# Pools and shared banks of the w_in stage divided by the end of their tiles, a bias added as columns, and gMLP transfers issued by GpSimd

## The chip, the cores and the metric

The kernel runs on one core of one Trainium2 chip. A core has TensorE (PE: matmuls and transposes into PSUM, eight banks of 2 KB per partition), VectorE (DVE), ScalarE (ACT), GpSimd (POOL) and SyncE (SP, which here only issues DMAs). The engines run side by side, each in its own program order; an instruction whose input or space isn't ready holds everything behind it on its engine. The metric is the device time of one execution in microseconds (us). A program's time is the median of its runs.

## The reference, cut to what matters

One layer over two token streams, 512 latent tokens and 128 context tokens, which the kernel holds as one block of T = 640 columns; a flag v (0 latent, 1 context) says which of two modulation vectors applies.

```python
mod = silu(c) @ w_mod + b_mod                       # once for c, once for c_ctx; six vectors of 2048
sh1, sc1, g1, sh2, sc2, g2 = split(mod, 6)
h = rmsnorm(x, norm1_g) * (1 + sc1) + sh1
p = h @ w_in                                        # 2048 x 5408
o_a = rwkv7_bidir(shift(p[..., :3360]))             # two delta-rule scans, 16 heads of 64
u, v = split(gelu(p[..., 3360:]), 2)                # gMLP, 8 groups of 128
v = layernorm_of_group(v) * gmlp_ln_g + gmlp_ln_b
o_b = u * (w_spatial @ v + b_spatial)
x = x + g1 * (concat(o_a, o_b) @ w_out)
h = rmsnorm(x, norm2_g) * (1 + sc2) + sh2
y = rmsnorm(x + g2 * ((silu(h @ w_gate) * (h @ w_up)) @ w_down), final_norm_g)
```

Results: the two streams after the last norm, and the context scan's final states. All is float32; large matmuls take each operand as a high and a low part and add three products.

## The kernel before, in words

Every array is transposed: 128 features on the partitions, 640 tokens along the row. The stages, in order of time: normalisation and the first two modulation vectors; **w_in**; **w_out** together with the scans (the recurrence over chunks of 64 tokens, one "hop" after another); the feed-forward layer in two stages (each a Strassen scheme of seven products in place of eight); the last norm.

*The w_in stage* (from about 150 us) makes 43 column blocks of p, 128 columns each, the first six already in the stage before. A block is four pieces of weights (raw, 256 KB each); each is cut into hi (ACT) and lo (DVE) and multiplied with h_hi and h_lo in groups of three matmuls of 320 columns into two of the three banks called big. `wide[0]` counts these groups: 192 at the stage's start, 1376 at its end. A finished block is copied to one of four buffers praw and goes to a generator: `take_r`, `take_v`, `take_k` prepare the scans, then `tail`, `solve` and `merge` invert the small triangular matrices of a head pair and direction (tiles TB, TF, M1, M2, A1_; PE's pblk, pM2, pT2) and store them with the scan's records in d_S; `take_gv` and `take_gu` make a gMLP group (lng, lnb, wsp, bsp are its loads; its product goes to d_o). `mod_all` makes the other four modulation vectors beside them: for each vector 16 pieces of 1 MB of weights (wt, through one buffer mraw), each multiplied in four matmuls of two rows (pm); piece n isn't let go before `wide[0]` is 192 + MODR * n. When 16 pieces are summed, ms (in the same buffer) is cleared by POOL, takes b_mod by eight DMAs, DVE adds the sums, PE transposes (ptm), and DVE copies the result to modc.

All these operations are recorded first (class `Op`, whose call is line 106, so that the stage's rows in the profile bear L106). `Lister` then writes them out: it keeps a clock for each engine, takes operations whose inputs are ready by its own estimates, and among them the task with the lower number of priority (gMLP and modulation have 5, the last). The order on each engine is fixed by this, including SP's DMAs. When w_in's products are all listed, the rest is written in a second run, `plan.run(last=True)`, outside the fixed order: the framework merges these instructions with those of the next stage by its own estimates.

*Space.* Tiles come from pools, and a pool has one piece of memory. When a stage's pools are closed, the next stage's pools lie in the same memory, and a tile there waits for the last user of every pool that it overlaps, not only of the tile that lay at its place. In w_in all working tiles of the left side are in three pools: bk, bp and gs; the four banks of its small PE results (slots, tags g0 to g3, used for pblk, psp, ptm and the like) are one pool pk; the modulation's bank is a tile of pm_. In w_out the space of bk, bp and gs is taken by x1T (the residual, loaded transposed by PE's pxT and then added to), by ol and oh (low and high part of d_o) and, over h_hi and h_lo, by the scan's records rec; the banks of pk by the pools pu, po (pxT's) and py.

*The w_out stage* here begins with the gMLP half: `wout_b` loads ol for rows 8 to 11 of d_o, then for each of 16 output tiles two half products of 12 matmuls (L1305 to L1307, banks pbig, two of them), which DVE adds onto x1T times the vector g1 (modc[2], L1318).

## Time and profile before

| | us |
|---|---|
| median of three runs | 3212.35 (3209.28 to 3218.95) |
| the profiled execution's own time | 3210.99 |
| its span, first to last instruction | 3209.2 |
| mean granted TensorE clock | 0.984 |
| PE busy | 3097.7 (97% of the span) |
| weight loads of PE | 2878.0 (90%) |
| DVE busy | 2328.3 (73%) |
| ACT busy | 1448.3 (45%) |
| POOL busy | 1256.2 (39%) |

Busy times say little of a stage: the prediction below reads the profile by stretches of time. A row of the time order gives start, duration, engine, line, operation, the tile written <- the tiles read, sizes and a count, and in brackets how long the engine stood idle before it and what ended that. "SPq" is a DMA issue on SP's queue.

### The profile page before, as it was taken

The page shows a single profiled execution, that of the slowest core. Times are in us where ns is not written, and L with a number is a line of the kernel's source. Part 1 is how long each engine was busy: PE and PEld are TensorE (multiplying, and loading weights), DVE is VectorE, ACT ScalarE, POOL GpSimd, SP SyncE. Part 2 cuts the span into 40 slices and gives each one's busy share as a digit, 9 for nine tenths or more (in the row PEclk, how much of TensorE's full clock was granted, in tenths as well). Part 3 has the DMA queues.
Part 4 walks back from the last instruction along what each step waited for, and adds up shares of the span by engine and source line. Part 5 has one row for each costly group of instructions (what it writes and reads, how often), then busy time and mean ns, then how long its engine had stood idle before and what let it go on. Part 6 is the DMA issues. An engine that isn't in the chain of part 4 may idle for free. (4 is left out here: it accounts for less than half of the span.)

```text
span 3209.2 us, 73753 instructions
## 1 busy us (share of the span) xinstructions
PE 3097.7 (97%) x28892; PEld 2878.0 (90%) x28892; DVE 2328.3 (73%) x4118; ACT 1448.3 (45%) x3169; POOL 1256.2 (39%) x1102
## 2 busy tenths in 40 slices
PE   7999999999997999999899999999999999999996
PEld 4888888888885877799899999999999999999996
DVE  5567676866765667557887777877778777877787
ACT  4245454555543433346544444444444444444365
POOL 1001222222220123210465666566656645555543
PEclk9999999999997999999999999999999999999998
DMA  9768888788797677356334334434343354554453
GB/s 349 241 186 245 207 228 229 200 239 228 193 249 236 205 226 240 116 156 187 100 119 126 118 109 129 126 108 123 118 123 120 107 183 145 169 164 130 124 171 122
DMA packets 746412, 553.02 MB, mean 172 GB/s; under 512 B 142128, under 2 KB 682768, under 8 KB 737232
## 3 DMA queue, kind: packets, MB, share of 16 engines
q1 hardware_dynamic: 733104, 534.52, 56.1%
q0 software_dynamic: 10624, 13.23, 1.8%
q8 instruction: 227, 3.72, 0.5%
q14 instruction: 121, 0.99, 0.1%
q10 hardware_dynamic: 2336, 0.57, 0.1%
HBM read 438.77 MB, written 111.69 MB: 172 GB/s over the span
## 5 line engine op out<-in xcount | busy, mean ns | idle before, releaser
L1875 PE MATMUL P<-xo,lo 128*128 128x320 f32 x2352 | 728.2, 310 | 7.5 <-DVE lo L1663 7.5
L1873 PE MATMUL P<-xo,hi 128*128 128x320 f32 x2352 | 728.1, 310 | 2.2 <-ACT hi L1662 2.2
L1874 PE MATMUL P<-xo,hi 128*128 128x320 f32 x2352 | 728.1, 310 | 0.0
L1663 DVE TENSOR_TENSOR lo<-raw,hi 128x512 fp32r<-128x512 f32 x532 | 504.3, 955 | 172.7 <-ACT hi L1662 170.9
L1662 ACT CAST hi<-raw 128x512 fp32r<-128x512 f32 x532 | 330.3, 622 | 505.5 <-PE P L1874 434.1
L1875 PEld LDWEIGHTS P<-xo,lo 128*128 128x128 f32 x2352 | 442.7, 188 | 8.0 <-DVE lo L1663 8.0
L1873 PEld LDWEIGHTS P<-xo,hi 128*128 128x128 f32 x2352 | 442.6, 188 | 2.4 <-ACT hi L1662 2.4
L1874 PEld LDWEIGHTS P<-xo,hi 128*128 128x128 f32 x2352 | 442.6, 188 | 0.0
L1773 POOL TENSOR_TENSOR raw<-raw 128x512 f32<-128x512 f32 x252 | 412.8, 1641 | 17.3 <-DVE lo L1663 4.1
L1875 PE MATMUL P<-xd,lo 128*128 128x320 f32 x1232 | 383.5, 311 | 5.6 <-DVE lo L1663 5.6
L106 PE MATMUL big<-h_hi,hi 128*128 128x320 f32 x1184 | 387.7, 327 | 0.7 <-DVE early L580 0.7
L1873 PE MATMUL P<-xd,hi 128*128 128x320 f32 x1232 | 383.3, 311 | 5.2 <-ACT P L2171 3.1
L1874 PE MATMUL P<-xd,hi 128*128 128x320 f32 x1232 | 382.1, 310 | 0.1
L106 PE MATMUL big<-h_lo,hi 128*128 128x320 f32 x1184 | 364.5, 308 | 0.0
L106 PE MATMUL big<-h_hi,lo 128*128 128x320 f32 x1184 | 364.4, 308 | 0.0
L1773 POOL TENSOR_TENSOR t<-raw 128x512 f32<-128x512 f32 x84 | 134.3, 1598 | 460.2 <-DMA raw<-in_w_ffn_up_dram 366.7
L1662 ACT CAST hi<-rawd 128x512 fp32r<-128x512 f32 (+1 forms) x288 | 165.0, 585 | 229.9 <-PE P L1874 144.4
L106 PEld LDWEIGHTS big<-h_hi,hi 128*128 128x128 f32 x1184 | 222.5, 188 | 35.4 <-issue 28.7
L1663 DVE TENSOR_TENSOR lo<-rawd,hi 128x512 fp32r<-128x512 f32 (+1 forms) x288 | 217.7, 764 | 49.4 <-ACT hi L1662 47.1
L1873 PEld LDWEIGHTS P<-xd,hi 128*128 128x128 f32 x1232 | 232.6, 189 | 8.8 <-ACT P L2171 5.6
L1875 PEld LDWEIGHTS P<-xd,lo 128*128 128x128 f32 x1232 | 232.4, 189 | 8.7 <-DVE lo L1663 8.4
L1874 PEld LDWEIGHTS P<-xd,hi 128*128 128x128 f32 x1232 | 232.6, 189 | 0.3 <-DVE xd L1926 0.3
(402 smaller groups left out, 6413.2 us busy)
## 6 DMA issues: line engine op xcount, KB each, us to landing
wt<-in_w_mod_dram SPq DMA_DIRECT2D x96, 1024.0 KB
raw<-in_w_ffn_gate_dram SPq DMA_DIRECT2D x182, 256.0 KB
raw<-in_w_ffn_up_dram SPq DMA_DIRECT2D x182, 256.0 KB
rec<-d_S SPq DMA_DIRECT2D x80, 576.0 KB
raw<-in_w_in_dram SPq DMA_DIRECT2D x166, 256.0 KB
rawd<-in_w_ffn_down_dram SPq DMA_DIRECT2D x128, 256.0 KB
raw<-in_w_out_dram SPq DMA_DIRECT2D x96, 256.0 KB
xd<-d_os SPq DMA_DIRECT2D x66, 320.0 KB
```

The lines of the kernel that those rows point to most:

```text
L106: self.eng, self.run = eng, lambda: fn(*args, **kw)
L1662: S.copy(hi[:, 0:nk], raw[:, 0:nk])
L1663: V.tensor_sub(lo[:, 0:nk], raw[:, 0:nk], hi[:, 0:nk].bitcast(F32))
L1773: G.tensor_tensor(out=o[:, 0:nk], in0=p[:, 0:nk], in1=q[:, 0:nk], op=ALU.subtract)
L1873: TE.matmul(ps, hi[:, k, :], xk[:, 0, :], start=f, stop=False)
L1874: TE.matmul(ps, hi[:, k, :], xk[:, 1, :], start=False, stop=False)
L1875: TE.matmul(ps, lo[:, k, :], xk[:, 0, :], start=False, stop=l)
```

## The change

Three things. (1) The three pools bk, bp and gs become four, bl, bx, bm and br, into which a table (`Homes`) sorts the tags; pk becomes pk1 (g0, g1) and pk2 (g2, g3), and after the last w_in product `slots.bar` lets the second run use g2 and g3 alone. (2) The bias of the four later modulation vectors is loaded once at the start as columns (bcols, 64 more rows of rowC) and added when the transposed sums are copied to modc; the sums are copied from their bank by ACT into a buffer praw; MODR is 16.8 in place of 18.0. (3) The gMLP loads and stores are issued by GpSimd (oG) in place of SP (oQ).

```diff
@@ -47,7 +47,7 @@
-MODR = 18.0
+MODR = 16.8
@@ -187,7 +187,11 @@
 
 
     def __init__(self, pool, tag, bufs):
-        self.pool, self.idle, self.busy = pool, [f"{tag}{i}" for i in range(bufs)], {}
+        self.pool, self.idle, self.busy, self.barred = pool, [f"{tag}{i}" for i in range(bufs)], {}, ()
+
+    def bar(self, tags):
+        self.barred = tags
+        self.idle = [t for t in self.idle if t not in tags]
 
@@ -202,7 +206,20 @@
         return t
 
     def done(self, t):
-        self.idle.append(self.busy.pop(id(t))[0])
+        tag = self.busy.pop(id(t))[0]
+        if tag not in self.barred:
+            self.idle.append(tag)
+
+
+class Homes:
+
+
+    def __init__(self, rest, *homes):
+        self.rest, self.of = rest, {tag: pool for pool, tags in homes for tag in tags.split()}
+
+    def tile(self, shape, dtype, name, tag=None, **kw):
+        t = dict(tag=tag) if tag else {}
+        return self.of.get(tag or name, self.rest).tile(shape, dtype, name=name, **t, **kw)
 
 
 def queue(q):
@@ -371,6 +388,7 @@
     prm = cp.tile([P, NPRM], F32, name="prm")
     modc = {g: cp.tile([P, KB, 2], F32, name=f"modc{g}") for g in (2, 3, 4, 5)}
     cT = cb.tile([P, 2 * KB + 32], F32, name="cT")
+    bcols = cb.tile([P, 4, KB], F32, name="bcols")
 
     d_o = dp.tile([KB, P, T], F32, name="d_o")
     d_x1 = dp.tile([KB, P, T], F32, name="d_x1")
@@ -453,11 +471,12 @@
         crow = p0.tile([32, P], F32, name="crow")
         nc.scalar.dma_start(crow[0:16, :], c.rearrange("o (r p) -> (o r) p", p=P))
         nc.scalar.dma_start(crow[16:32, :], c_ctx.rearrange("(r p) -> r p", p=P))
-        rowC = p0.tile([48, P], F32, name="rowC")
+        rowC = p0.tile([112, P], F32, name="rowC")
         for g in range(2):
             nc.scalar.dma_start(rowC[16 * g:16 * g + 16, :],
                                 b_mod[:, g * D:(g + 1) * D].rearrange("o (r p) -> (o r) p", p=P))
         nc.scalar.dma_start(rowC[32:48, :], norm1_g[0].rearrange("(r p) -> r p", p=P))
+        nc.scalar.dma_start(rowC[48:112, :], b_mod[:, 2 * D:6 * D].rearrange("o (r p) -> (o r) p", p=P))
         th0 = p0.tile([32, P], F32, name="th0")
         S.activation(th0, crow, AF.Tanh, scale=0.5)
         V.tensor_scalar(th0, th0, 0.5, 0.5, op0=ALU.mult, op1=ALU.add)
@@ -469,11 +488,12 @@
         V.tensor_copy(cT3[:, :, 0], pc[:, 0, 0:16])
         V.tensor_copy(cT3[:, :, 1], pc[:, 0, 16:32])
         pp = ps0.tile([P, 4, P], F32, tag="pt", name="pp")
-        TE.transpose(pp[:, 0, 0:48], rowC, ident[0:48, 0:48])
+        TE.transpose(pp[:, 0, 0:112], rowC, ident[0:112, 0:112])
         bmod = p0.tile([P, 2, KB], F32, name="bmod")
         V.tensor_copy(bmod, pp[:, 0, 0:32].rearrange("p (g k) -> p g k", g=2))
         V.tensor_scalar_add(bmod[:, 1, :], bmod[:, 1, :], 1.0)
         V.tensor_copy(prm[:, C_N1:C_N2], pp[:, 0, 32:48])
+        V.tensor_copy(bcols, pp[:, 0, 48:112].rearrange("p (g k) -> p g k", g=4))
 
         xnT = p0.tile([P, KB, T], F32, name="xnT")
         ss, rs = (p0.tile([P, NT], F32, name=n) for n in ("ss", "rs"))
@@ -620,7 +640,10 @@
 
     v3 = lambda ap: ap.rearrange("p (c t) -> p c t", t=CH)
 
-    bk, bp, gs = (hp.enter_context(tc.tile_pool(name=n, bufs=1)) for n in ("bk", "bp", "gs"))
+    bl, bx, bm, br = (hp.enter_context(tc.tile_pool(name=n, bufs=1)) for n in ("bl", "bx", "bm", "br"))
+    bk = bp = gs = Homes(br, (bl, "A1_ TB TF M1 GB0 GB1 GB2 GB3 mraw lng lnb wsp"),
+                         (bm, "praw vt2 u2 wspT gmn gva grs rk"),
+                         (bx, "scan1 waM c0l c0c w0h kah ka1 mx2 mx3 gi zr wlr wh wl"))
     db = hp.enter_context(tc.tile_pool(name="db", bufs=2, space=DRAM))
     BQ = nc.gpsimd
     hsl = lambda h: slice(64 * h, 64 * h + 64)
@@ -974,9 +997,9 @@
 
     def take_gv(vv, g, read):
         lng, lnb, wsp = (gs.tile([P, P], F32, tag=n, name=n) for n in ("lng", "lnb", "wsp"))
-        yield oQ.dma_start(lng, gmlp_ln_g[0, g].partition_broadcast(P))
-        yield oQ.dma_start(lnb, gmlp_ln_b[0, g].partition_broadcast(P))
-        yield oQ.dma_start(wsp, w_spatial[0, g])
+        yield oG.dma_start(lng, gmlp_ln_g[0, g].partition_broadcast(P))
+        yield oG.dma_start(lnb, gmlp_ln_b[0, g].partition_broadcast(P))
+        yield oG.dma_start(wsp, w_spatial[0, g])
         yield from gelu2(vv)
         yield slots.free
         pw = slots.tile([P, 4, P], F32, "pw")
@@ -1006,7 +1029,7 @@
 
     def take_gu(uu, g, read):
         bsp = gs.tile([P, P], F32, tag="wsp", name="bsp")
-        yield oQ.dma_start(bsp, b_spatial[0, g].partition_broadcast(P))
+        yield oG.dma_start(bsp, b_spatial[0, g].partition_broadcast(P))
         yield from gelu2(uu)
         vt, wspT = vts[g]
         sp = bp.tile([P, NT, P], F32, tag="u2", name="sp", bufs=1)
@@ -1019,7 +1042,7 @@
             slots.done(ps)
         yield oV.scalar_tensor_tensor(out=uu, in0=uu, scalar=0.5, in1=sp.rearrange("p t n -> p (t n)"),
                                      op0=ALU.mult, op1=ALU.mult)
-        yield oQ.dma_start(d_o[8 + g], uu)
+        yield oG.dma_start(d_o[8 + g], uu)
 
     A1_ = bp.tile([P, 2, NCH, 32], F32, name="A1_")
     TB = bp.tile([P, 2, NCH, 2, 32], F32, name="TB")
@@ -1128,28 +1151,25 @@
     def mod_all():
         n = 0
         for g in (2, 4, 3, 5):
-            pm = pm_.tile([P, 512], F32, tag="pmod", name=f"pm{g}")
             for kb in range(KB):
                 yield lambda: wide[0] >= 192 + MODR * n
                 n += 1
                 quad = bk.tile([P, 4, 512], F32, tag="mraw", name="wt", bufs=1)
                 yield oQ.dma_start(quad.rearrange("p j n -> p (j n)"), w_mod[0, kb * P:(kb + 1) * P, g * D:(g + 1) * D])
-                yield [oT.matmul(pm[32 * j:32 * j + 2, :], cT[:, 2 * kb:2 * kb + 2], quad[:, j, :],
+                yield [oT.matmul(pmod[32 * j:32 * j + 2, :], cT[:, 2 * kb:2 * kb + 2], quad[:, j, :],
                                 start=(kb == 0), stop=(kb == KB - 1), tile_position=(0, 32 * j)) for j in range(4)]
-            ms = bk.tile([P, 4, 512], F32, tag="mraw", name=f"ms{g}", bufs=1)[:, 0, :]
-            yield oG.memset(ms, 0.0)
-            for j in range(4):
-                for v in range(2):
-                    yield oQ.dma_start(ms[32 * j + v:32 * j + v + 1, :],
-                                      b_mod[:, g * D + 512 * j:g * D + 512 * j + 512])
-            for j in range(4):
-                yield oV.tensor_add(ms[32 * j:32 * j + 2, :], pm[32 * j:32 * j + 2, :], ms[32 * j:32 * j + 2, :])
+            yield prw.free
+            pr = prw.tile([P, T], F32, "praw")
+            ms = pr[:, 0:512]
+            yield oS.copy(ms, pmod)
             yield slots.free
             pt = slots.tile([P, 4, P], F32, "ptm")
             yield [oT.transpose(pt[:, cb, :], ms[:, cb * P:(cb + 1) * P], ident) for cb in range(4)]
+            prw.done(pr)
             src = pt.rearrange("p cb (j r) -> p j cb r", r=32)
             for v in range(2):
-                yield oV.tensor_copy(modc[g].rearrange("p (j cb) v -> p j cb v", cb=4)[:, :, :, v], src[:, :, :, v])
+                yield oV.tensor_tensor(out=modc[g].rearrange("p (j cb) v -> p j cb v", cb=4)[:, :, :, v], in0=src[:, :, :, v],
+                                      in1=bcols[:, g - 2, :].rearrange("p (j cb) -> p j cb", cb=4), op=ALU.add)
             slots.done(pt)
 
     qA, qB, qS, qM, qT, qR, qX, qZ = [], [], [], [], [], [], [], []
@@ -1236,7 +1256,10 @@
         (qR if b == 4 else qA).append(blocks[b][1](pr, lambda: None))
     pex.close()
     pb = pbx.enter_context(tc.tile_pool(name="pb", bufs=3, space=PSUM))
-    pk = pbx.enter_context(tc.tile_pool(name="pk", bufs=1, space=PSUM))
+    pk1, pk2 = (pbx.enter_context(tc.tile_pool(name=n, bufs=1, space=PSUM)) for n in ("pk1", "pk2"))
+    pk = Homes(pk2, (pk1, "g0 g1"))
+    pmod = pm_.tile([P, 512], F32, tag="pmod", name="pmod")
+    V.memset(pmod, 0.0)
     big, slots = Ring(Kept(pb), "big", 3), Slots(Kept(pk), "g", 4)
     with tc.manual_schedule(engines={getattr(mybir.EngineType, e) for e in ("PE", "DVE", "Activation", "Pool", "SP")}):
         plan = Lister(wides())
@@ -1254,6 +1277,7 @@
         plan.add(queue(qB), 5)
         plan.add(mod_all(), 5)
         plan.run()
+    slots.bar(("g0", "g1"))
     plan.run(last=True)
     assert not (qT or qA or qB or qS or qM or qE or qR or qX or qZ) and len(merged) == 2 * NPAIR
     hp.close()
```

The order of instructions moves with it in the whole w_in stage; three places follow. Lines from 394 on stand 18 to 24 lower after the change: L1305 to L1307 become L1329 to L1331, L1563 becomes L1587, L1558 becomes L1582, L1291 becomes L1315, L1318 becomes L1342.

TensorE, before, behind the last w_in product and the last merges (numbers tell apart the buffers; wt is a piece of modulation weights, pxT the next stage's first transposes):

```order
L106 MATMUL pm5_11403<-wt_13688,cT_87 2x512 x4
L106 MATMUL psp_13902<-wspT_13739,vt2_13761 128x128
L106 MATMUL pm5_11403<-wt_13872,cT_87 2x512 x4
L106 MATMUL psp_13902<-wspT_13739,vt2_13761 128x128 x3
L106 MATMUL psp_13908<-wspT_13739,vt2_13761 128x128
L1377 MATMUL swap_14433<-I2_68,s0_14023 64x64 x4
L1437 MATMUL w_ps_14442<-ST_14438,rec_14015 64x64 x4
L106 MATMUL pm5_11403<-wt_13897,cT_87 2x512 x4
L106 MATMUL ptm_13931<-ident_63,ms5_13917 128x128 x4
L1563 MATMUL pxT_14049<-ident_63,x1T_13968 128x128 x4
```

TensorE, after, from the last w_in product on (big over h is a w_in product, big over oh or ol one of w_out):

```order
L106 MATMUL big_13510<-h_hi_368,lo_13537 128x320
L106 MATMUL pM2_13763<-TB_1638,GB_12019 32x32 x20
L1329 MATMUL big_14019<-oh_13988,hi_14022 128x320
L1330 MATMUL big_14019<-ol_13989,hi_14022 128x320
L1331 MATMUL big_14019<-oh_13988,lo_14023 128x320
L106 MATMUL pT2_13786<-TF_13512,M2_13762 32x32
L1329 MATMUL big_14019<-oh_13993,hi_14022 128x320
L1330 MATMUL big_14019<-ol_13994,hi_14022 128x320
```

The modulation's last products and ptm have moved ahead of the last w_in product (their rows stand some 30 rows above this piece); the first products of w_out follow it directly, with the last merge and the last two gMLP groups spread among them.

SP, before, the queue where the next stage's loads begin again (rec: the scan's records; ms: the modulation's bias rows; ol: the low part of d_o):

```order
L106 DMA wt_13897<-in_w_mod_dram 128x2048
L106 DMA d_o_88<-praw_13525 128x640
L1371 DMA s0_14025<-in_state_rwkv_dram 128x2x64
L397 DMA raw_14290<-in_w_out_dram 128x4x128
L1366 DMA rec_14423<-d_S_94 128x2x576
L106 DMA ms5_13917<-in_b_mod_dram 1x512 x8
L1558 DMA x1T_13962<-in_x_sample_dram 128x4x128
L1558 DMA x1T_13962<-in_x_prompt_dram 128x128
```

SP, after, where the first ol stands:

```order
L1582 DMA x1T_13927<-in_x_prompt_dram 128x128
L1582 DMA x1T_13926<-in_x_sample_dram 128x4x128
L1315 DMA ol_13989<-d_o_89 128x640
L1315 DMA ol_13994<-d_o_89 128x640
L106 DMA raw_13005<-in_w_in_dram 128x4x128
L1315 DMA ol_13999<-d_o_89 128x640
L106 DMA wt_13010<-in_w_mod_dram 128x2048
L106 DMA raw_13040<-in_w_in_dram 128x4x128
```

Before, ten of the 16 x1T pairs and all ol stand behind the last modulation piece and its bias rows. After, the 16 pairs and the first four ol stand among the last w_in loads (raw over in_w_in); seven of those are still to come behind the first ol, and 17 single x1T loads stand together ahead of the last but one. The loads and stores of the gMLP groups are gone from this queue.

VectorE, after, behind the last additions of the merge (vt2, gq, praw and sp belong to gMLP groups, gl to the gate, lo to the weights of w_out; L1342 frees a w_out bank):

```order
L106 TENSOR_TENSOR vt2_13631<-vt2_13631,lnb_13505 128x640
L106 TENSOR_TENSOR gq_13815<-gq_13815,praw_13150 128x640
L1354 COPY J2_13960<-I2_68 128x64
L1358 TENSOR_TENSOR gl_13963<-gl_13963,gh_13962 128x640
L417 TENSOR_TENSOR lo_14115<-raw_14113,hi_14114 128x512
L106 SCALAR_TENSOR_TENSOR praw_13150<-gq_13815,praw_13150 128x640
L1342 SCALAR_TENSOR_TENSOR x1T_13929<-big_14019,modc2_83,x1T_13929 128x320
L106 TENSOR_TENSOR sp_13825<-psp_13826,bsp_13813 128x512
L106 TENSOR_TENSOR sp_13825<-psp_13832,bsp_13813 128x128
L1342 SCALAR_TENSOR_TENSOR x1T_13929<-big_14020,modc2_83,x1T_13929 128x192
```

Before, the gMLP operations of this stretch were all done ahead of the first L1318; now they stand between the additions of the first five w_out tiles.

## The prediction

> **What bounds the kernel now.** I read the page's row of slices first, to find where TensorE (PE) is not full, then the windows of that place, then the order of time inside it.
>
> ```profile
> PE   7999999999997999999899999999999999999996
> PEclk9999999999997999999999999999999999999998
> ```
>
> Each digit is a slice of 80 us. PE is full nearly everywhere; the start and the end are not touched by this change. The one hole inside is slice 13 (963 to 1043 us), and the granted clock falls there too. The windows around it show its size:
>
> ```profile
> 150.00:960.00 810.00, 803.93 (x10466) 708.69 (x10465) 564.82 (x1189) 412.51 (x890) 180.26 (x289) 1.00 0.82 220
> 960.00:973.40 13.40, 11.31 (x151) 9.69 (x148) 8.33 (x14) 8.15 (x19) 3.31 (x5) 1.00 1.05 203
> 973.40:984.00 10.60, 8.12 (x328) 5.63 (x328) 7.48 (x15) 3.53 (x8) 1.02 (x1) 0.96 0.62 186
> 984.00:1030.20 46.20, 30.54 (x322) 19.53 (x322) 23.15 (x45) 11.76 (x23) 3.76 (x6) 0.53 0.77 261
> 1030.20:1059.00 28.80, 28.80 (x202) 27.65 (x199) 13.31 (x31) 9.89 (x22) 0.00 (x0) 1.00 0.73 215
> ```
>
> Columns: window, its length, busy us of PE, weight load, VectorE (DVE), ScalarE (ACT), GpSimd (POOL), then clock, DMA share, GB/s. From 150 to 960 us PE loses 6.1 of 810 us: the w_in stage is bound by PE, and moving work off other engines inside it gains next to nothing. From 1030.2 the w_out stage runs PE at 100%. Between 973.4 (the last w_in product has just ended) and 1030.2 (the second w_out tile begins) lie 56.8 us, most of them at a clock of 0.53. PE's work in them, at full clock, is 8.12 x 0.96 = 7.8 plus 30.54 x 0.53 = 16.2, together 24.0 us. So **32.8 us** are idle or slow time: the most that filling this hole can give. What ends it:
>
> ```profile
> 973.70 1.02 PE L106 MATMUL pm<-wt,cT 128*2 128x512 f32 x2 [1.07 <-DMA wt<-in_w_mod_dram]
> ...
> 1009.22 1.89 PE L106 MATMUL pm<-wt,cT 128*2 128x512 f32 x8 [0.86 <-DMA wt<-in_w_mod_dram]
> 1011.20 0.52 POOL L106 MEMSET ms<- 128x512 f32 x1 [13.35 <-PE pm L106]
> 1011.75 2.32 SPq L106 DMA_DIRECT2D ms<-in_b_mod_dram x8
> 1013.51 2.84 DVE L106 TENSOR_TENSOR ms<-pm,ms 2x512 f32<-2x512 f32 x4 [4.51 <-DMA ms<-in_b_mod_dram]
> 1016.45 1.09 PE L106 MATMUL ptm<-ident,ms 128*128 128x128 f32 x4 [5.35 <-DVE ms L106]
> 1017.58 0.26 DVE L106 COPY modc<-ptm 128x16 f32<-128x16 f32 x2 [1.23 <-PE ptm L106]
> 1017.91 1.75 SPq L1291 DMA_DIRECT2D ol<-d_o x4
> 1017.98 1.09 PE L1563 MATMUL pxT<-ident,x1T 128*128 128x128 f32 x4 [0.44 <-DVE modc L106]
> ...
> 1030.26 0.41 PE L1305 MATMUL big<-oh,hi 128*128 128x320 f32 x1
> ```
>
> Five pieces of the modulation product (pm) run after w_in, each behind its 1 MB weight load; then memset, eight bias loads, adds, transposes (ptm), copies to modc. Only then do pxT (the w_out stage's first transposes) and the loads ol start, though neither reads modc: they wait for the space, since pxT's bank lies in the pool of ptm and ol's memory in pools that hold ms.
>
> **The change, part by part.**
>
> *Pools and banks.* Nothing computed changes; what moves is which wait releases the w_out stage. In the new order shown above PE's first w_out product stands right behind the last w_in product; the loads ol stand among the last w_in loads. All ten x1T pairs and four ol that came after 1014 us now load before w_in ends. PE then finds ready work where it idled, and its clock should stay at 1.00. Bounds: 0 to 32.8 us; I take the whole and subtract below what takes the idle's place.
>
> *Bias as columns, and MODR 16.8.* Piece n (0 to 63) is let go at product group 192 + 18.0n, now 192 + 16.8n, of 1376 groups: the last at 1250 instead of 1326. The five late pieces move in among the products; their PE time stays the same, and is in the 24.0 us. Per vector group go one memset, eight DMAs and four adds (2.84 us of DVE, above), and an ACT copy of the bank comes (0.59 us, as in the first stage). Three of the four groups lie inside the PE-bound stretch: nothing, either way, under a tenth of the 6.1 us that PE loses there. The fourth is the chain shown above, part of the hole.
>
> ```profile
> L544 ACT COPY ms<-pm x10: 580/587/599, 24.4 to 128.8; 128x512 f32<-128x512 f32 x10
> ...
> L472 PE MATMUL pp<-ident,rowC x1: 338/338/338, 9.4 to 9.4; 48*128 48x48 f32 x1
> L554 DVE TENSOR_TENSOR mc<-mc,bmod x10: 155/164/169, 28.8 to 133.9; 128x8 f32<-128x8 f32 x6, 128x4 f32<-128x4 f32 x4
> ```
>
> At the start one more load and a taller transpose stand before pp (9.4 us), whose result bmod is first read at 28.8 us: 19 us of cover, so 0; without cover about 1 us (one ACT issue, one copy).
>
> *gMLP transfers by GpSimd.* 5 x 8 = 40 DMAs leave SP's queue and join POOL's. SP's issue slots gate nothing in 150 to 960 us, so this gains 0. On POOL each wait for its slot or its product holds what stands behind it: the merges' own transfers.
>
> ```profile
> POOL d_S L106 <- ACT TF L106: 16.1, 2, 11.7
> d_S<-TF POOLq DMA_DIRECT2D x16, 320.0 KB, 6.2
> ```
>
> POOL already waits up to 11.7 us at a store and lands one in 6.2 us while PE loses next to nothing, so I take 0; the other end is the rival below.
>
> **What takes the idle's place.** First, VectorE:
>
> ```profile
> 967.32 0.68 DVE L399 TENSOR_TENSOR lo<-raw,hi 128x512 fp32r<-128x512 f32 x1
> 968.21 0.49 DVE L106 TENSOR_SCALAR gq<-gq 128x640 f32<-128x640 f32 x1
> 971.74 0.82 DVE L106 TENSOR_TENSOR vt<-vt,lng 128x640 f32<-128x640 f32 x1
> 976.55 2.04 DVE L106 TENSOR_TENSOR TF<-pblk,TB 32x320 f32<-32x320 f32 x4
> 979.01 0.69 DVE L106 TENSOR_TENSOR sp<-psp,bsp 128x512 f32<-128x512 f32 x1 [0.42 <-PE psp L106]
> 980.69 0.29 DVE L106 TENSOR_TENSOR sp<-psp,bsp 128x128 f32<-128x128 f32 x1 [0.26 <-PE psp L106]
> 1040.25 0.55 DVE L1318 SCALAR_TENSOR_TENSOR x1T<-big,modc,x1T 128x320 f32<-128x320 f32 x1 [1.26 <-PE big L1307]
> 1041.94 0.68 DVE L1318 SCALAR_TENSOR_TENSOR x1T<-big,modc,x1T 128x192 f32<-128x192 f32 x2 [1.14 <-PE big L1307]
> 1044.48 0.55 DVE L1318 SCALAR_TENSOR_TENSOR x1T<-big,modc,x1T 128x320 f32<-128x320 f32 x1 [1.26 <-PE big L1307]
> ```
>
> The rest of the last gMLP groups now runs beside w_out, and every w_out half needs a DVE addition (L1318) before its bank comes free (two banks). By the new order of DVE, from the last TF additions to the addition of the fifth w_out tile's first half stand: 14 full-width operations x 0.82 = 11.5, the four TF 2.0, two tensor_scalar of 0.49 and two tiny ones 1.3, sp twice 2.0, conversions lo 4 x 0.68 = 2.7, tile additions 4 x 1.23 + 0.55 = 5.5, the gate's preparation (three full-width and a small copy) 2.6: 27.6 us. PE's side:
>
> ```profile
> 977.06 0.82 PE L106 MATMUL pM<-TB,GB 32*32 32x32 f32 x40
> 977.81 1.16 PE L106 MATMUL psp<-wspT,vt 128*128 128x128 f32 x8
> 978.90 0.81 PE L106 MATMUL pT<-TF,M 32*32 32x32 f32 x39
> 980.16 0.49 PE L106 MATMUL psp<-wspT,vt 128*128 128x128 f32 x2
> ...
> 959.12 0.60 PE L106 MATMUL pvt<-ident,praw 128*128 128x128 f32 x4
> ```
>
> A w_out tile takes 1044.48 - 1040.25 = 4.23 us; 4.5 of them 19.0, with pM, pT and two psp 4.9, and the last gMLP group's six transposes about 1.1 (four take 0.60): 25 us. DVE is some 2.6 us longer, and waits in between for ACT and POOL (gaps like the 0.26 and 0.42 above, some eight of them, so 2 to 3.4 us): PE is held about **5 us** (0 if the list interleaves well, 10 if the waits add up).
>
> Second, pT now waits for ACT's copies of pM with three products between: about **1.5 us** (0 to 3).
>
> Third, transfers:
>
> ```profile
> 900.00:973.40 73.40, 71.31 (x1034) 62.39 (x1033) 46.50 (x101) 31.95 (x68) 18.69 (x29) 1.00 0.88 236
> 950.00:960.00 10.00, 10.00 (x72) 8.93 (x71) 4.17 (x6) 4.08 (x9) 4.19 (x7) 1.00 0.99 310
> x1T<-in_x_sample_dram SPq DMA_DIRECT2D x16, 256.0 KB
> ol<-d_o SPq DMA_DIRECT2D x16, 320.0 KB
> ```
>
> The last 73 us of w_in must also carry ten x1T pairs (256 and 64 KB each) and four ol: 4.5 MB, and 7% more of the modulation's weights, some 0.7 MB. The best window reached 310 GB/s, the stretch 236, so 74 GB/s x 73.4 us = 5.4 MB fit at best. It just fits, with 17 x1T loads queued on SP ahead of one w_in load; I charge **3 us** (0 to 8).
>
> Sum: 32.8 - 5 - 1.5 - 3 = 23.3 us. The profiled execution took 3210.99 us (span 3209.2 and 1.8 around it), 1.4 under the median 3212.35 of the three runs shown: 3212.35 - 23.3 = **3189 us**.
>
> **The rivals.**
>
> *The cover is not there* (transfers and VectorE both at their far ends, since everything is pulled into one stretch): 32.8 - 10 - 3 - 8 = 11.8; and if a quarter of the 5.2 MB doesn't fit at all, another 1.3 MB at the 261 GB/s of 984 to 1030.2 us = 5 us: gains of 6.8 to 11.8, 3201 to 3206. For it: DMA share 0.88 and DVE's list longer than PE's. Against: a share of 0.99 with PE full (950 to 960 us).
>
> *The split frees nothing*: pxT and ol still wait for a last user of their space; then only the bias chain (1011.2 to 1016.3, 5 us) goes: 3207. Against: the new order puts both ahead of the gMLP tail.
>
> *Slower: POOL's queue holds the merges.* Each of the eight gMLP stores on POOL waits for a DVE product; behind it stand the merge's transfers TB, and PE waits for TB in a fixed order (pblk). If 6 us of each came through to PE, 48 us would be lost in 200 to 984 us: 3189 + 48 = 3237. It ends slower from 4.1 us each (33 us, the 23 and 10 more). Against: the 11.7 us wait above came while PE lost only what the hole shows. The Trainium skill speaks for this rival: "SBUF — State Buffer", § SBUF: two separate sides, says that the descriptors of a DMA issued by GpSimd are written by GpSimd's own cores, which VectorE's fast-mode operations lock out, and gives 3.1 us beside such an operation for a transfer of 0.62 us. By that (an estimate) each of the 40 would be 2.5 us late, five in a group 12.5, enough to bring this rival on: 3237 in place of 3189; the trace, where POOL's transfers ran beside a DVE busy 70% of 150 to 960 us and PE lost 6.1, does not bear that out, and the chance stays low.
>
> **Chances.** Forecast 0.74 (gains of 12 to 33 us); thin cover 0.14, half of it over 9.6 us; split frees nothing 0.05; POOL's queue 0.05; a gain beyond the ceiling, by the 2.1 us idle in 960 to 973.4, 0.02. A difference under 0.3% (9.6 us) can't be told from none here: faster 0.74 + 0.07 + 0.02 = 0.83, same 0.07 + 0.05 = 0.12, slower 0.05. The range takes in the bounds: 3212.35 - 32.8 - 2.1 = 3177 at one end, a gain of 9 in the thin cover's middle at the other: 3177 to 3203.
>
> **What would show it.** Right: no slice under 9 between the stages, clock 1.00 throughout; the first w_out product within 3 us of the last w_in product; ptm ahead of it; x1T and ol issued ahead of the last w_in load; PE's waits there DVE's, a few us. The last w_in product comes later than 973 us (some 984), since five pm pieces and most of the merge now lie before it. Wrong: PE waiting for ACT hi (its raw late) or wt over 8 us before the hand-over; pblk waiting for TB; a DVE at 9 or more for long after the hand-over with PE behind it.

## The result, and the profile after

| | before | after |
|---|---|---|
| median of five runs, us | 3212.35 (3209.28 to 3220.51) | 3197.86 (3193.28 to 3199.92) |
| profiled execution, us | 3210.99 | 3198.94 |
| its span, us | 3209.2 | 3197.2 |

The ratio of after to before is 0.9945, with a 95% interval of 0.9927 to 0.9963: 14.5 us less, where 23.3 were forecast. Measured once more beside the experiments (e8_after, below) it was 0.9950 (0.9937 to 0.9964).

The page's rows of slices of the kernel after:

```profile
PE   7999999999998999999899999999999999999996
PEclk9999999999999999999999999999999999999998
```

The 7 of PE and the 7 of its clock that stood in slice 13 are an 8 and a 9 now: the hole is smaller, not gone. The windows of 10 us there, after (columns as in the prediction):

```profile
930.00:940.00 10.00, 8.06 (x54) 7.54 (x52) 3.60 (x6) 6.44 (x14) 5.32 (x10) 1.00 1.08 231
940.00:950.00 10.00, 5.30 (x22) 3.60 (x23) 3.81 (x7) 3.21 (x6) 0.00 (x0) 0.66 0.99 226
950.00:960.00 10.00, 10.00 (x180) 8.68 (x179) 4.73 (x9) 2.94 (x8) 1.05 (x1) 1.00 1.00 289
960.00:970.00 10.00, 8.58 (x166) 7.85 (x164) 7.77 (x12) 3.79 (x7) 0.71 (x2) 1.00 0.94 232
970.00:980.00 10.00, 5.68 (x45) 3.74 (x47) 1.18 (x3) 0.94 (x2) 0.00 (x0) 0.67 0.67 225
980.00:990.00 10.00, 10.00 (x168) 9.22 (x162) 4.71 (x7) 3.78 (x7) 4.01 (x7) 0.99 0.62 154
990.00:1000.00 10.00, 10.00 (x193) 8.99 (x190) 4.74 (x11) 4.30 (x9) 1.74 (x2) 1.00 0.27 62
1000.00:1010.00 10.00, 8.40 (x106) 7.72 (x99) 7.92 (x15) 4.26 (x9) 2.49 (x4) 0.71 0.85 229
1010.00:1020.00 10.00, 8.64 (x60) 8.24 (x60) 8.22 (x16) 5.48 (x12) 1.63 (x3) 0.95 0.72 224
1020.00:1030.00 10.00, 9.55 (x67) 8.89 (x66) 8.68 (x17) 5.21 (x11) 1.18 (x1) 1.00 0.97 327
```

What a window loses is its length less PE's busy time times the clock. The rows up to 980 us lose 1.9 + 6.5 + 0 + 1.4 + 6.2 = **16.1 us**, still inside w_in; the three from 1000 us on lose 4.0 + 1.8 + 0.5 = **6.3 us**, behind the hand-over to w_out. Before, 32.8 us were lost in the hole and 2.1 idle just ahead of it. 34.9 less 22.4 is 12.5; the spans differ by 12.0. What ended the waits, in the order of time on PE, after:

```profile
944.70 1.89 PE L106 MATMUL pmod<-wt,cT 128*2 128x512 f32 x8 [6.35 <-DMA wt<-in_w_mod_dram]
...
974.32 1.89 PE L106 MATMUL pmod<-wt,cT 128*2 128x512 f32 x8 [5.75 <-DMA wt<-in_w_mod_dram]
...
999.50 0.30 PE L106 MATMUL big<-h_hi,lo 128*128 128x320 f32 x1
...
1000.69 0.41 PE L1329 MATMUL big<-oh,hi 128*128 128x320 f32 x1
...
1002.85 0.22 PE L106 MATMUL pT<-TF,M 32*32 32x32 f32 x2 [1.46 <-DVE TF L106]
...
1016.17 0.30 PE L106 MATMUL pw<-ident,wsp 128*128 128x128 f32 x1 [1.36 <-DMA wsp<-in_w_spatial_dram]
```

The first w_out product comes 1.2 us after the last w_in product: the hand-over is what the prediction said. But PE waited 12.1 us in all for two pieces of modulation weights. SP's queue, after:

```profile
929.94 0.41 SPq L106 DMA_DIRECT2D wt<-in_w_mod_dram  x1
...
951.12 0.50 SPq L1582 DMA_DIRECT2D x1T<-in_x_sample_dram  x1
...
965.87 0.56 SPq L1582 DMA_DIRECT2D x1T<-in_x_prompt_dram  x1
966.53 1.57 SPq L106 DMA_DIRECT2D wt<-in_w_mod_dram  x1
```

The piece needed at 944.70 was issued at 929.94 and took 14.8 us. That needed at 974.32 was issued at 966.53; its buffer had been free since 958.5, but 18 x1T loads and one raw held the queue from 951.12 on, for 15 us. The load was issued 8.0 us late, which is more than the wait of 5.75 us, and then took 7.8 us.

### The profile page after: what moved, and what is told of

The parts are those of the page before. It is cut to its first block, busy times and chain, and to the rows that moved or that the text cites. A ratio compares the mean times of both kernels' runs of the same rounds, so it can differ in the third digit from the quotient of the medians.

```text
span 3197.2 us, 73695 instructions
## 1 busy us (share of the span) xinstructions
PE 3091.0 (97%) x28892; PEld 2876.7 (90%) x28892; DVE 2333.2 (73%) x4104; ACT 1450.4 (45%) x3173; POOL 1276.2 (40%) x1138
## 4 chain that ended last, share of the span: by engine, by line
PE 85%; DMA 5%; issue 4%; DVE 4%; ACT 1%; POOL 1%; SPq 0%; DVEq 0%; ACTq 0%; POOLq 0%
PE big L106 16%; PE P L1899 15%; PE P L1897 15%; PE P L1898 15%; DMA wt<-in_w_mod_dram 2%; PE pmod L106 2%; PE big L1329 2%; PE pG L106 1%; PE pblk L106 1%; PE big L1330 1%; PE big L1331 1%; PE y_ps L1432 1%; PE u_ps L1476 1%; DMA opd<-d_op 1%; DVE lo L1687 1%
## 5 line engine op out<-in xcount | busy, mean ns | idle before, releaser
L1687 DVE TENSOR_TENSOR lo<-raw,hi 128x512 fp32r<-128x512 f32 x532 | 517.2, 979 | 163.4 <-ACT hi L1686 161.3
```

Of the source, the lines that this page charges most:

```text
L1687: V.tensor_sub(lo[:, 0:nk], raw[:, 0:nk], hi[:, 0:nk].bitcast(F32))
```

## The experiments

All are the changed kernel with one edit. Two theories. **T, transfers:** x1T and ol, pulled ahead of the hand-over, hold up the last loads of wt. **V, VectorE:** the gMLP tail behind the hand-over sets the time, and waits for wt only take the place of later ones.

### Which part brings the gain

**e8_after**, the changed kernel unedited.

> The changed kernel once more, for its time beside these runs and to see whether its waits are the same in a second profile: 3194 to 3201, waits for wt of 10 to 15 us between 930 and 980 us in two places, a wait of 1 to 2 us for TF at the hand-over.

3200.10, as expected; waits for wt of 5.97 and 4.33 us at the same two places, TF 1.45. The wait that the first profile puts down to wsp is one for VectorE's addition here:

```profile
1017.22 0.30 PE L106 MATMUL pw<-ident,wsp 128*128 128x128 f32 x1 [2.23 <-DVE x1T L1342]
```

**e4_no_cols**, the second part undone.

```diff
-MODR = 16.8
+MODR = 18.0
...
-            yield oS.copy(ms, pmod)
+            ms = bk.tile([P, 4, 512], F32, tag="mraw", name=f"ms{g}", bufs=1)[:, 0, :]
+            yield oG.memset(ms, 0.0)
+            for j in range(4):
+                for v in range(2):
+                    yield oQ.dma_start(ms[32 * j + v:32 * j + v + 1, :],
+                                      b_mod[:, g * D + 512 * j:g * D + 512 * j + 512])
```

> Edit to the changed kernel: the second part undone (bias rows loaded into ms, MODR 18.0), with pools divided and gMLP on GpSimd as changed. Five modulation pieces and the chain of ms then stand behind the last w_in product, pxT beside them, and the first w_out product behind those. Theory T: the loads of wt come behind x1T and the loads of w_out, and PE, with nothing else ahead of it, waits for each: 20 us or more between the last w_in product and the first w_out product, 3203 to 3213, so the parts are only worth something together. The other reading (the pools alone bring the gain, the modulation's place is of no account): 3195 to 3200.

3211.56, ratio to before 0.9996 (0.9985 to 1.0007): the whole gain is gone. Its w_out products (first and last start in the row of the tile oh) begin at 1024.2, as late as before (1023.4):

```profile
L1327 PE MATMUL big<-oh,hi x256: 302/412/633, 1024.2 to 1349.9; 128*128 128x320 f32 x128
```

**e7_no_pools**, the first part undone.

```diff
-    bl, bx, bm, br = (hp.enter_context(tc.tile_pool(name=n, bufs=1)) for n in ("bl", "bx", "bm", "br"))
+    bk, bp, gs = (hp.enter_context(tc.tile_pool(name=n, bufs=1)) for n in ("bk", "bp", "gs"))
...
-    pk = Homes(pk2, (pk1, "g0 g1"))
+    pk = pbx.enter_context(tc.tile_pool(name="pk", bufs=1, space=PSUM))
...
-    slots.bar(("g0", "g1"))
```

> Edit to the changed kernel: the first part undone (three pools and one pool of banks as before, all four banks to the end), the bias columns, MODR 16.8 and GpSimd's gMLP transfers kept. ol, most x1T and all pxT stand behind the last gMLP group again, and the scans' first hops ahead of them. The rival of the prediction in which the split frees nothing put this at 3207. Theory T: the waits for wt shrink, since fewer x1T loads stand among them (one load of wt has seven ahead of it), and a hole of 15 to 25 us opens behind the last w_in product: 3200 to 3210. If the pools are of no account: 3195 to 3200.

3211.13, 0.9987 (0.9979 to 0.9996). Its windows:

```profile
930.00:980.00 50.00, 46.68 (x673) 40.62 (x672) 23.75 (x42) 16.33 (x32) 8.39 (x15) 0.97 0.64 159
980.00:990.00 10.00, 6.98 (x182) 6.31 (x182) 7.70 (x14) 4.82 (x10) 2.71 (x4) 0.77 0.51 133
990.00:1020.00 30.00, 9.62 (x67) 7.45 (x65) 17.25 (x30) 7.26 (x14) 4.39 (x6) 0.50 0.65 215
```

With most x1T and all ol behind the hole again, w_in loses 4.7 of these 50 us (DMA share 0.64); but from 990 to 1020 us 25 of 30 us are lost. So the first two parts bring 14.5 us together and 1 to 4 each without the other.

**e12_nobar**, all four small banks to the end.

```diff
-    slots.bar(("g0", "g1"))
```

> Edit to the changed kernel: the second run keeps all four small banks (the last gMLP group may take g0 and g1), with the SBUF pools still divided. pxT then stands behind the scans' first products, and w_out's tiles, which need x1T, behind pxT; the first products of w_out still stand behind the last w_in product, two banks deep. If the division of the banks carries as much as that of the pools: PE runs out after the first w_out tile and waits some 10 to 20 us for the last gMLP group: 3205 to 3213. If the SBUF pools alone carry the gain: 3196 to 3202. My reading is the first. Waits for wt as in the changed kernel, 12 to 15 us.

3219.62, 1.0022 (1.0009 to 1.0034), a little slower than before, and slower than either expectation. In the row of oh:

```profile
L1328 PE MATMUL big<-oh,hi x256: 302/413/633, 996.0 to 1358.3; 128*128 128x320 f32 x128
```

The first w_out product is early and the last one 13 us later than after (1358.3 against 1345.2): the first pxT comes at 1026.7 in place of 1007.1, so that the first tiles can't be finished, and PE ran 5.19, 3.09 and 5.64 us of the three 10 us from 1000 us. Beside the divided SBUF pools, this one line of the division of the banks is worth some 20 us. The banks divided with the SBUF pools left whole was not run.

**e3_gmlp_sp**, the third part undone.

```diff
-        yield oG.dma_start(d_o[8 + g], uu)
+        yield oQ.dma_start(d_o[8 + g], uu)
```

(and so the four loads.)

> Edit to the changed kernel: the 40 gMLP loads and stores go back to SP. In this order the last modulation piece stands at product group 1330 in place of 1362, and the merges and the last gMLP group all stand ahead of the last w_in product. The prediction costed the move at nothing. Theory P (POOL's queue costs something): faster by 4 us or more, with POOL's waits at TB and d_S shorter. Theory T: the loads of wt still stand among x1T, with a gMLP store waiting on SP among them as well; within 5 us of the changed kernel, 3193 to 3203, with 8 to 16 us of waits for wt. Theory V: the gMLP work ends ahead of the hand-over, so PE loses nothing behind it: 3190 to 3193.

3195.74, 0.9947 (0.9934 to 0.9959): no difference from the changed kernel that can be told.

### What the last 16 us of w_in are lost to

**e1_halves**: each piece in two halves, two buffers.

```diff
-                quad = bk.tile([P, 4, 512], F32, tag="mraw", name="wt", bufs=1)
+            pair = bk.tile([P, 2, 512], F32, tag="mraw", name="wt", bufs=2)
...
+                    yield lambda: wide[0] >= 192 + MODR / 2 * n
+                    ahead.append(load(n))
+                    yield ahead[-1][1]
```

> Edit to the changed kernel: each 1 MB piece of modulation weights becomes two halves of 512 KB in two buffers of half the size, the next one loading beside the products of the one before, with MODR 16.0; the last piece then stands at w_in product group 1220 of 1376 in place of 1362, ahead of the x1T loads on SP's queue. Theory T (transfers): from 930 to 980 us the changed kernel loses 16 us of full-clock time (length less busy time times clock), 12.1 of it idle for wt and the rest a lowered clock behind those waits, because the loads of wt stand behind x1T and ol on SP's queue and share the DMA engines with them. With wt out of the way, PE's waits for wt fall below 2 us, the clock stays at 1.00 to the hand-over, and the time falls by 12 to 16 us: 3182 to 3186. Theory V (VectorE): what holds PE is the tail of gMLP work beside the first w_out tiles; the waits for wt only take the place of waits after the hand-over, which grow by as much: 3194 to 3199.

3256.63: neither theory, but a cost that I had not counted. Its page:

```profile
PE 3157.1 (97%) x28892; PEld 2877.8 (88%) x28892; DVE 2312.6 (71%) x4104; ACT 1448.2 (45%) x3173; POOL 1276.5 (39%) x1138
```

66.1 us more of PE than after's 3091.0, in the same number of instructions: the two products of a half, beside each other, take as long as the four of a whole piece, so that 64 pieces of 1.04 us (66.6) are paid twice. Less these 66.1 us the span of 3254.1 would be 3188.0, 9 us under the changed kernel's 3197.2, and no wait for wt is left after 900 us: that is T's side, but by subtraction, not by a run.

**e5_columns** and **e6_columns_late**: halves of 256 columns for all four groups; MODR 16.0 and 16.8.

```diff
+            half = bk.tile([P, 4, 256], F32, tag="mraw", name="wt", bufs=2)
...
+                yield [oT.matmul(pmod[32 * j:32 * j + 2, s], cT[:, 2 * kb:2 * kb + 2], half[:, j, :],
```

> The run with the halved pieces took 66 us more of PE's time, since a half there held two of the four column groups of PE, and two products beside each other take as long as four; its 3256.6 less that 66.1 is 3190.5. Here a half is 256 columns for all four groups, so PE's time is that of the changed kernel; MODR 16.0, the last half at product group 1222 of 1376, ahead of all but one of the x1T loads. Theory T (the loads of wt are late behind and beside x1T): no wait for wt above 1 us after 900 us; of the 16 us lost from 930 to 980 us at most 8 stay, as a wait for TB whose transfers share the DMA engines with x1T (4.1 us and a lowered clock in the run with halves): 3183 to 3190, 8 to 15 under the changed kernel. Theory V (the VectorE tail at the hand-over sets the time): within 4 us of the changed kernel.

> As the run with column halves at MODR 16.0, with 16.8: the last seven halves stand at product groups 1219 to 1270, among the x1T loads on SP's queue, ten of these ahead of the last but none and six behind it; the hand-over has the same order. Theory T: waits for wt of 2 to 6 us in all, and 2 to 8 us slower than with 16.0, faster than the changed kernel by 3 to 11. Theory V: the same as with 16.0.

3217.27 and 3220.83: slower than the changed kernel, against both theories' numbers. Rows of e5, PE's groups, windows and order of time:

```profile
L106 PE MATMUL pmod<-wt,cT 128*2 128x256 f32 x1024 | 78.9, 380 | 9.7 <-DMA wt<-in_w_mod_dram 9.7
```

```profile
300.00:500.00 200.00, 195.92 (x2870) 167.55 (x2867) 140.64 (x309) 106.75 (x237) 52.98 (x87) 0.99 0.90 228
500.00:700.00 200.00, 193.17 (x2839) 164.67 (x2838) 133.54 (x290) 102.07 (x228) 54.62 (x88) 0.99 0.92 235
...
940.00:950.00 10.00, 5.02 (x35) 4.76 (x33) 1.84 (x3) 2.40 (x4) 4.93 (x9) 0.89 1.04 174
950.00:960.00 10.00, 6.99 (x35) 6.80 (x36) 5.45 (x8) 7.03 (x17) 0.00 (x0) 0.60 1.16 246
```

```profile
953.01 0.63 PE L106 MATMUL big<-h_hi,hi 128*128 128x320 f32 x1 [7.99 <-ACT praw L106]
```

The sum closes: PE is busy 15.0 us longer (3106.0 against 3091.0), which the expectation had put at nothing, 10.6 of it in the products of the first row (68.3 us in the changed kernel); 300 to 700 us lose 14.8 instead of 2.7, among it the 9.7 us of waits for wt in the first row; and 11.3 + 2.8 us are lost around the hand-over instead of 22.4: 15.0 + 12.1 - 8.3 = 18.8, beside the 17 to 19 measured. No wait for wt is left after 900 us in e5, as T said, and nothing was given back behind the hand-over, against V; but at a DMA share of 1.04 to 1.16 another wait of 8 us came up in its place. e6 has three waits for wt there, of 2.1 to 3.1 us, and is 3.6 us slower than e5 by the medians, as T expected, though the intervals of the two overlap (0.9997 to 1.0018 and 1.0005 to 1.0025).

**e2_x1_act**: x1T issued by ScalarE.

```diff
-                            nc.sync.dma_start(xc[:, t0:t0 + n, :],
+                            nc.scalar.dma_start(xc[:, t0:t0 + n, :],
```

> Edit to the changed kernel: the 32 x1T loads are issued by ScalarE in place of SP; PE's order around the hand-over is the same. It tells the place in SP's queue from the sharing of the DMA engines. In the changed kernel the load behind the wait of 5.75 us was issued 8 us after its buffer was free, with 17 x1T loads ahead of it, and landed in 7.8 us; the load behind the wait of 6.35 us was issued 2.9 us after its buffer was free and took 14.8 us to land. Theory T, as a matter of the queue: the wait of 5.75 us goes below 1 with its lowered clock, some 8 us, and the other stays: 3188 to 3192. Theory T, as a matter of the DMA engines alone: both waits stay, 3196 to 3200. Theory V: 3196 to 3200, with the wait of VectorE's TF at the hand-over longer.

3205.99, outside all three. Only the first wait for wt was left (5.1 us); the load behind the second was issued at 972.25, when the x1T loads were over. But now they held ScalarE; its order of time, then PE's:

```profile
967.67 0.27 ACT L106 COPY wspT<-pw 128x128 f32<-128x128 f32 x1 [11.89 <-DMA x1T<-in_x_prompt_dram]
```

```profile
968.80 1.28 PE L106 MATMUL pblk<-M,TB 32*32 32x32 f32 x40 [7.91 <-ACT M L106]
```

The Trainium skill, "DMA: Bandwidth & Descriptors", § Issuing engines are not separate DMA queues, says that all engines' DMAs run on the same 16 DMA engines and that another issuer saves only issuing time. This run agrees; but the time of issue, which that section calls usually small beside the transfer, was the 15 us above on SP, and here ScalarE stood 11.9 us with x1T loads in front of it.

**e9_hold4** and **e10_hold4_sp**: x1T held back behind wt. e10 has the gMLP transfers on SP besides.

```diff
+                        if m >= 4:
+                            V.tensor_copy(x1T[m][:, 0:T:LAT], modc[5][:, 0:2, 0])
                         for t0, src in ((0, x_sample[0]), (4, x_prompt[0])):
```

> Edit to the changed kernel: for the output tiles 4 to 15, VectorE writes two columns of x1T out of the last modulation vector before its load, so that 24 of the 32 x1T loads (3.9 MB) wait for that vector and stand behind the last load of wt on SP's queue; PE's order is the same up to the first w_out product, and no product is larger or smaller. Theory T, in the queue's form: the second wait for wt (5.75 us, its load issued 8 us late behind 17 x1T loads) falls below 1 us with the lowered clock behind it; the first (6.35 us; its load stands behind four x1T pairs and ol as before) keeps 3 to 6 us; x1T then loads beside w_out, a tile of 320 KB in some 1.3 us at 245 GB/s where w_out takes 4.2 us a tile, so pxT waits for none but perhaps the fifth tile: 3185 to 3191 beside 3198 to 3200. Theory V: what is gained before the hand-over is lost behind it, 3196 to 3201. If the x1T loads are late then: waits of pxT for x1T after 1010 us, 3198 or more.

> The same hold on x1T, with the gMLP transfers back on SP (the order in which the merges and all but one gMLP product stand ahead of the last w_in product). Without the hold that order took 3195.7, and lost 14 us of full-clock time from 930 to 970 us, 5.6 of it idle for wt and for wsp, whose loads had 10 and 12 x1T loads ahead of them, the rest lowered clock. Theory T: 5 to 11 us of that go: 3185 to 3191, with losses of 2 to 3 us behind the hand-over as without the hold. Theory V: the same 3195 to 3198, since VectorE's tail was already small there. If gMLP's transfers on GpSimd matter by themselves (the prediction said 0), this run and the one with the hold alone differ by more than 5 us.

3191.45 and 3191.68, both 0.9937 (0.9925 to 0.9949 and 0.9923 to 0.9951), just above T's 3185 to 3191: the lowest of all, 6 to 9 us under the changed kernel by the medians and 3 to 4 by the ratios to before, though the intervals overlap with its own. PE's order of time, the row of oh and the windows behind the hand-over in e9:

```profile
942.81 1.89 PE L106 MATMUL pmod<-wt,cT 128*2 128x512 f32 x8 [6.24 <-DMA wt<-in_w_mod_dram]
```

```profile
L1329 PE MATMUL big<-oh,hi x256: 302/412/633, 990.9 to 1335.3; 128*128 128x320 f32 x128
```

```profile
990.00:1000.00 10.00, 8.54 (x107) 7.76 (x108) 7.66 (x13) 4.45 (x9) 2.49 (x4) 0.66 0.92 235
1000.00:1010.00 10.00, 8.14 (x47) 7.48 (x47) 7.51 (x13) 4.49 (x10) 1.63 (x3) 0.84 0.80 267
1010.00:1020.00 10.00, 10.00 (x71) 9.66 (x69) 7.55 (x16) 5.19 (x10) 1.19 (x1) 0.98 0.80 243
1020.00:1030.00 10.00, 9.40 (x67) 8.88 (x67) 8.34 (x18) 3.15 (x8) 0.60 (x1) 1.00 0.78 242
```

The second wait for wt is gone and the first is there to 0.1 us, as T said of the queue. With PE's order unchanged the first w_out product comes 9.8 us earlier (990.9 against 1000.7) and the last one 9.9 earlier; 1.9 us of that lead stand already at the first wait (942.81 against 944.70), so some 8 go with the second. Behind the hand-over these windows lose 4.4 + 3.2 + 0.2 + 0.6 = 8.4 us, in ten more us than the 6.3 above, but from the first w_out product to the last both kernels take 344 us: V would have given back all. The hold takes x1T out of the queue and off the DMA engines at once, so it doesn't tell these two apart. That e9 and e10 agree says again that the issuer of the gMLP transfers is of no account.

**e11_hold0**: the hold for all 16 tiles.

```diff
+                        V.tensor_copy(x1T[m][:, 0:T:LAT], modc[5][:, 0:2, 0])
                         for t0, src in ((0, x_sample[0]), (4, x_prompt[0])):
```

> The hold for all 16 tiles: no x1T load stands ahead of the last load of wt; ol and w_in's own weights do, as before. With 24 loads held the first wait for wt stayed (6.24 us; its load took 14.9 us from issue to product, with four x1T pairs and ol among the transfers in the 20 us before, the DMA engines at a share of 1.02 to 1.09). Theory T, in the form that the DMA engines' time is what runs out there: 1.3 MB less before that load, so that wait falls to 0 to 3 us, and 3184 to 3190 if no pxT is late for it (the first x1T then loads some 15 us ahead of its product). If the wait is ol's doing alone (SP held at ol until 926 to 930 us, behind the scan's transfers d<-mx): it stays at 5 to 6 us, and 3189 to 3194.

3197.26, 0.9953 (0.9937 to 0.9968), slower than both forecasts. PE and SP in order of time:

```profile
935.80 0.63 PE L106 MATMUL big<-h_hi,hi 128*128 128x320 f32 x1 [2.46 <-ACT hi L106]
...
943.18 1.89 PE L106 MATMUL pmod<-wt,cT 128*2 128x512 f32 x8 [2.60 <-DMA wt<-in_w_mod_dram]
```

```profile
924.00 1.33 SPq L1315 DMA_DIRECT2D ol<-d_o  x3
925.42 1.32 SPq L106 DMA_DIRECT2D raw<-in_w_in_dram  x1
926.80 1.56 SPq L1315 DMA_DIRECT2D ol<-d_o  x1
928.46 0.60 SPq L106 DMA_DIRECT2D wt<-in_w_mod_dram  x1
```

Without any x1T ahead, that load of wt still took 14.7 us, and PE waited 5.1 us, half of them for w_in's raw behind the same ol. So the first wait is not x1T's. It goes with the four ol (1.3 MB) issued in the 4 us ahead of it, behind SP's stand at the first of them; a place for ol that is free earlier wasn't tried, so this part is argued. The first w_out product is as early as in e9 (991.2), but the last one 3.6 us later (1338.9): in these two profiles holding the first tiles too costs more than it brings.

## Why the prediction was right, and where its size was off

- **The hole and its release: right.** The first w_out product follows within 1.2 us; ptm (992.84), x1T and ol stand ahead. It needs the banks beside the SBUF pools (e12), the two together (e7) and the bias as columns (e4); the prediction had them as one step but did not say that a half alone brings next to nothing.
- **VectorE 5 and pT 1.5: right in sum, by luck**, 6.5 forecast and 6.3 lost behind the hand-over. pT's wait is 1.46 us, as forecast. VectorE was over-sized: of waits for its additions only one shows, 2.23 us in e8 and put down to wsp (1.36) in the first profile, with 0.45 us later for vt. The rest, some 3.4 us, is a lowered clock, which the forecast did not have.
- **Transfers 3 (0 to 8): the term that was mis-sized.** 16.1 us were lost where w_in's last transfers run, twice the upper bound; 12.1 of them waits for wt, most of the rest the clock behind these. The step that failed is "it just fits": it took the room from the best window's rate, 310 GB/s, over 236. From 930 to 960 us, at a DMA share of 0.99 to 1.08, the windows moved 226 to 289 GB/s. The share in the prediction's own row was 0.88: 12% of 73.4 us, 8.8 us, at 236 / 0.88 = 268 GB/s is 2.4 MB of room for 5.2 MB, and the 2.8 MB over would take 10 us. That is an estimate (its 0.7 MB of modulation weights is too much as well: six pieces were issued in that stretch before, and 7% of them is 0.4), and not a proof that the total was too large: in the last 20 us before the hand-over the share was 0.62 and 0.27. What the rows show is when the loads came and in what order. The 17 queued x1T loads were named, but priced into the 3 us; they stood ahead of the load behind the second wait (e9 holds them back and is rid of it). That the first wait is ol's was argued, not shown. So the last w_in product came at 999.5 instead of some 984.
- **gMLP transfers 0: right** (e3, e10). POOL waited 20.2 us at one store d_o, and no wait of PE for TB came of it. The estimate that the prediction took from the Trainium skill, "SBUF — State Buffer", § SBUF: two separate sides, 40 transfers 2.5 us late each, would show in e3 if it stood on PE's path; nothing did.
- **Bias columns at the start 0: nothing that shows.** The first w_in product starts at 161.8 us before and 163.9 after, 160.8 to 163.9 in the other runs.
- **Sum.** 3.0 for transfers instead of 16.1 is 13.1 of optimism; the 2.1 us ahead of the hole, which the forecast had left out, came back. 23.3 - 13.1 + 2.1 = 12.3, by the profiled executions 12.0, by the medians 14.5.
- **Signs and rivals.** Of its signs of being wrong one showed, waits for wt of over 8 us before the hand-over (12.1 in all, neither alone), and of those of being right three failed: slice 13 is an 8, the clock fell in four of the windows above (0.66 to 0.95), and PE's longest waits are for transfers, not for VectorE. The gain lies nearer to that of the rival "the cover is not there" (up to 11.8) than to 23.3: its half on transfers came, and more than fully; its half on VectorE did not. That the time is within the range owes as much to the range's width as to the sum.

## What to carry to other kernels

The best rate that any window shows (310 GB/s here) is not the rate of the next full stretch (226 to 289 at a share of about 1): estimate the room from the share of the DMA engines that is free, and then look at the queue, since what stands ahead of a load in its queue delays its issue (8.0 us here). Work pulled over a stage's end by freeing its space starts where the old stage's last loads still run, so hold back what isn't needed first (e9: 24 loads, behind twelve copies of two columns) rather than split the loads that are late (e5). Where two parts of a change release the same wait, either alone can measure as nothing.

## What the runs showed of the hardware

A short wait can be followed by a lowered clock that costs more than the wait. Windows of the kernel after:

```profile
974.32:980.40 6.08, 6.08 (x61) 4.14 (x61) 1.58 (x3) 0.94 (x2) 0.00 (x0) 0.51 0.54 178
...
1000.70:1002.85 2.15, 0.69 (x3) 0.46 (x4) 2.07 (x5) 0.80 (x2) 0.87 (x2) 1.00 0.79 231
...
1004.00:1008.00 4.00, 4.00 (x52) 3.86 (x52) 3.57 (x6) 1.47 (x3) 1.52 (x2) 0.52 0.92 190
1008.00:1011.00 3.00, 3.00 (x14) 2.96 (x12) 1.34 (x3) 1.39 (x3) 0.00 (x0) 0.51 1.04 395
```

The 5.75 us wait is followed by 6.1 us at a clock of 0.51, which cost 3.0 more; the wait of 1.46 us at 1002.85 by some 7 us at 0.51, 3.4 more, and the same pair stands in e8, e9 and e11 (waits of 1.3 to 1.5 us, clocks of 0.66 to 0.68 in their windows of 10 us). It is no fixed price: at the next wait of that stretch, that of pw, the clock stayed at 1.00 behind 1.36 us in the kernel after and behind 2.23 us in e8, and stood at 0.50 for 2.5 us behind 1.84 us in e9. What decides between these isn't shown. The Trainium skill, "TensorE: Matmul & The Clock Gate", § What's actually happening, has the clock halve after an idle window of about 3.4 us and return after as long a busy one. The half rate agrees; but here PE worked 1.8 of the 3.3 us from 1000.7 to 1004 (0.69 in the row above, the rest 32 x 32 and 128 x 320 products), and the return took about two such windows. Behind the first wait for wt, of 6.35 us, it took 4.7 us (944.70 to 949.40, at 0.50).
